# w_down of a ConvFFN by Strassen's seven block products for 16 of its 22 k tiles, and whole rows of x in the opening

## The chip, the cores and the metric

The kernel runs on one core of a Trainium2 chip. The metric is the device time of one execution in microseconds (us), lower is better. PE is the matmul engine (TensorE), DVE the VectorE, ACT the ScalarE, POOL the GpSimd, and SP the engine that issues the DMAs. PSUM has 8 banks here, each 128 partitions by 512 float32.

## What is computed

One decoder block on x of 512 tokens by 1024, in float32. Attention with a top-k choice and a recurrence run side by side, are merged and added to x; then comes a convolutional feed-forward part (FFN), and a last normalisation. The part that the change is about:

```python
    h = h + ga1 * jnp.dot(merged, w_out[l])
    xn = rms_norm(h, g_ffn[l]) * (1.0 + sc2) + sh2
    up = causal_dwconv(jnp.dot(xn, w_up[l]), conv_ffn_w[l], conv_ffn_b[l])
    val, gte = jnp.split(up, 2, axis=-1)
    h = h + ga2 * jnp.dot(jax.nn.silu(gte) * val, w_down[l])
return rms_norm(h, g_final)
```

w_up is 1024 by 5632 and w_down 2816 by 1024, so w_down has 22 tiles of 128 rows (k tiles).

## The kernel before, in words

**Number format.** Each float32 operand of a large product is split into a high part (an ACT copy to the matmul's type) and a low part (a DVE subtraction of that copy): `split`. A product is then three matmul passes, high by high, high by low and low by high (`mm3`, L530). A pass of 128x512 is the unit of work on PE in this text. Tiles with an h at the end of the name are high parts, with an l low parts (`wh`, `wl`; `dh`, `dl`; `acth`, `actl`).

**Order.** The program is recorded as operations with costs and ranks. A planner (`Plan.order`) lists them greedily by rank within a fixed number of slots for each kind of buffer, and writes out a fixed order for each engine. The engines then run these orders and wait for each other by semaphores. There are 3 slots of 1 MB for raw weights ("W"), 6 for split weights of 128x1024 ("w"), 75 tiles of 128x512 ("t") and the 8 banks ("b"). Everything that is loaded or stored goes through SP's queue in the planner's order.

**Opening.** x comes in as eight half rows of 256 KB (four row tiles `x`, two halves each), with the first block of w_ada (`wa`) between them. The squares of rows 2 and 3 go to ACT, the rows are scaled (`xs`), transposed on PE (L542), modulated, and multiplied with the first tiles of w_in (`w0h`, `w0l`). `WARM` groups of four transposes of the unit matrix stand on PE ahead of that. The modulation comes from dot products of w_ada with `crow`, one DVE instruction of 128x1024 each (L615).

**Middle.** w_in in tiles of 128 columns (8 k tiles, 24 passes each), attention, recurrence, w_o, w_out. `h1`, the residual after w_out, stays in SBUF as eight tiles (`xr_`).

**FFN.** Tile n of w_up (44 tiles, 22 loads of 1 MB, one for two tiles) is split (`wh`, `wl`), takes 24 passes of PE, and its bank goes through an ACT copy and two DVE multiply-adds for the convolution (`cv`, L471). A pair of tiles ends in a silu, a product, and the split into `acth` and `actl`. Behind the last tile, w_down runs k tile by k tile over eight banks (four row tiles t, two halves h): each load of 1 MB (`wd`) holds two k tiles, is multiplied by the gate `ga` on DVE, and split into `dh` and `dl`. The last five k tiles run bank by bank, so that the banks end one behind the other; the last bank is cut in two halves of 256 columns. Then each bank is added to h1, squared, scaled and stored.

Of the kernel before, what the change touches and what calls it, by code (L numbers as in the profile page):

```python
# [43 lines left out]
INFLATE = 1.19  # L44
HORIZON = 26
EARLY = 3
LAST = 5
# [4 lines left out]
WARM = 8  # L52
DOT1 = 13.6
SECOND = -25.0
LATER = 19.39
CLOCK = 12.7
RB = [3.28, 5.94, 7.96, 11.0, 13.85, 0.61]
SOON = [20.62, 17.45, 25.0, 11.19]
ISTEP = {1: 13, 2: 37.5, 3: 88.8}
IW = {1: 18, 2: 46.8, 3: 42.2}  # L60
ASTEP = {0: 76, 1: 93, 2: 126, 3: 145}
AW = [8, 13.5, 18.7, 30.4]
BUMP = [0.16, 0.81]
# [109 lines left out]
class Plan:  # L173
# [21 lines left out]
    def op(self, engs, reads, writes, emit, func=None, hold=(), n=1, tag="", follow=None):  # L195
# [25 lines left out]
        bufs += hold  # L221
# [15 lines left out]
    def order(self):  # L237
# [30 lines left out]
        table = [None]  # L268
# [127 lines left out]
def block_kernel(ctx: ExitStack, tc: tile.TileContext, x, cols, wada1, wada2, win0, win, wgate,  # L396
# [46 lines left out]
    def dma(dst, src, nbytes, reads=()):  # L443
        P.op({"sp": max(0.15, nbytes / 360e3)}, list(reads), [dst],
             lambda e: nc.sync.dma_start(real(dst), src() if callable(src) else src))

    def act(dst, src, func, bias=0.0, scale=1.0, accum=None, hold=()):
        n = width(src)
        cost = 0.04 + 0.00094 * n + 0.093 * sum(isinstance(v, (Buf, View)) for v in (bias, scale, accum))
# [12 lines left out]
    def tt(dst, a, b, op, engs=("dve",)):  # L462
        n = max(width(a), width(b))
        c = {"dve": 0.07 + 0.00104 * n, "pool": 0.03 + 0.00234 * n}
# [8 lines left out]
    def ts(dst, a, s1, s2, op0, op1=None, engs=("dve",)):  # L473
# [3 lines left out]
             "pool": 0.05 + 0.0014 * n}  # L477
# [96 lines left out]
    xt = [[t2(name="x") for _ in range(2)] for _ in range(TT)]  # L574
    for t in range(TT):
        for h in range(2):
            P.soft = -70.0 + 2 * t + h if t < 2 else -56.0 + 2 * t + h
            dma(xt[t][h], x[t * 128:(t + 1) * 128, h * 512:(h + 1) * 512], 1 << 18)
# [3 lines left out]
    for h in range(2):  # L582
# [4 lines left out]
        act(crow[:, h * 512:(h + 1) * 512], ps, AF.Copy)  # L587
    P.soft = None

    def rstd_of(halves, engs=("act", "dve")):  # L590
        parts = [small((128, 1), "ss") for _ in halves]
        ms = small((128, 1), "ms")
        for h, v in enumerate(halves):
            square(t2(name="junk")[:, :width(v)], v, parts[h], engs)
# [9 lines left out]
    def normed(halves, after=0.0, engs=("act", "dve")):  # L604
        r = rstd_of(halves, engs)
# [36 lines left out]
    xs = [normed(xt[t], LATER, ("act", "dve") if t < 2 else ("act",)) for t in range(TT)]  # L642
# [15 lines left out]
    for n in range(WARM):  # L658
        P.soft, P.after = -43.0, 3.7
        transposes(g0ps[-1], [ident] * 4)  # L660
    P.soft, P.after = None, 0.0
    n0 = len(G0) * 128
    for kt in range(KT):
        raw = buf("W", (128, 2, 1024), F32, "wa")
        if kt < 2:
            P.soft = -60.0 + 20.0 * kt
            dma(raw[:, 1, :], wada1[kt, :, 1, :], 1 << 19)
            P.soft = -58.0 + 20.0 * kt
            dma(raw[:, 0, :], wada1[kt, :, 0, :], 1 << 19)
# [446 lines left out]
    for t in range(TT):  # L1116
# [14 lines left out]
        h1.append(hv)  # L1131
# [23 lines left out]
    for n in range(2 * FT):  # L1155
        if n % 4 == 3 and ada_next < 16:
            ada_rest(ada_next)
            ada_next += 1
# [178 lines left out]
```

## Time and profile before

| | us |
|---|---|
| Median of 3 runs | 796.47 (796.18 to 796.88) |
| Profiled execution | 796.1 |
| Its span in the trace | 794.3 |
| First matmul of w_in starts, from the span's start | 17.34 |
| w_down's passes, alone on PE | 667.6 to 787.7 |

Columns "PE" and "PEld" are the matmuls and their weight loads, which overlap; matmuls are pipelined, so the duration of one is longer than the distance from its start to the next one's. The granted clock is a share of 2.4 GHz, TensorE's upper level; 0.50 is the lower one, 1.2 GHz. 1.8 us of the profiled execution lie outside the span.

### The profile page before, as it was taken

How to read it: one execution, taken by the hardware profiler on the slowest of the kernel's cores; microseconds unless marked ns; L12 is line 12 of the kernel's file. 1: busy time of each engine (PE TensorE's matmuls, PEld its weight loads, DVE VectorE, ACT ScalarE, POOL GpSimd, SP SyncE). 2: the span in 40 equal slices, each digit the busy share in tenths (PEclk: the TensorE clock that was granted, in tenths of full speed). 3: DMA queues.
4: the chain of work that ended last, by engine and by line, in shares of the span. 5: the costliest groups of instructions: out<-in, count | busy, mean ns of one | idle time of the engine just before them, and what ended most of it. 6: DMA issues, size and time to landing. Idle time of an engine off the chain costs nothing.

```text
span 794.3 us, 9871 instructions
## 1 busy us (share of the span) xinstructions
PE 775.3 (98%) x3608; PEld 645.3 (81%) x3608; DVE 595.8 (75%) x1144; ACT 439.2 (55%) x752; POOL 48.3 (6%) x69
## 2 busy tenths in 40 slices
PE   5999999999899999999999999999999999999996
PEld 5888888877777888888888888888888888888885
DVE  4997976999999998869866876665565698774034
ACT  6579935588799879635146644444444355232013
POOL 1000000014022051000010000000000000000000
PEclk8999999999999999999999999999999999999999
DMA  9974132321122451549740444333333224441002
GB/s 320 398 261 146 53 115 98 112 101 54 53 81 84 155 179 61 186 138 365 279 145 1 160 158 157 116 111 122 107 106 106 91 72 156 159 146 38 2 28 79
DMA packets 21298, 105.23 MB, mean 132 GB/s; under 512 B 2377, under 2 KB 4865, under 8 KB 10625
## 3 DMA queue, kind: packets, MB, share of 16 engines
q1 hardware_dynamic: 21248, 104.60, 36.6%
q8 instruction: 28, 0.46, 0.2%
q14 instruction: 22, 0.17, 0.1%
HBM read 102.47 MB, written 3.69 MB: 134 GB/s over the span
## 4 chain that ended last, share of the span: by engine, by line
PE 79%; DVE 11%; ACT 5%; issue 2%; DMA 1%; SPq 0%; POOLq 0%; POOL 0%; DVEq 0%; ACTq 0%
PE ps L530 78%; DVE sc L897 2%; DVE wl L466 2%; PE ps L542 2%; DVE m L896 1%; ACT l L459 1%; DVE sc L471 1%; DMA x<-in_x_dram 1%; ACT L459 1%; DVE h L854 1%; DVE q L471 1%; DVE rg L466 1%; ACT wh L459 1%; ACT gb L459 0%; DVE al L466 0%
## 5 line engine op out<-in xcount | busy, mean ns | idle before, releaser
L530 PE MATMUL ps<-yl,wh 128*128 128x512 f32 (+1 forms) x376 | 141.9, 377 | 0.3
L530 PE MATMUL ps<-yh,wh 128*128 128x512 f32 (+1 forms) x376 | 141.5, 376 | 0.0
L530 PE MATMUL ps<-yh,wl 128*128 128x512 f32 (+1 forms) x376 | 141.2, 375 | 0.0
L459 ACT ACTIVATE wh<-wr 128x1024 fp32r<-128x1024 f32 (+1 forms) x96 | 97.7, 1020 | 60.6 <-PE ps L530 46.6
L466 DVE TENSOR_TENSOR wl<-wr,wh 128x1024 fp32r<-128x1024 f32 (+1 forms) x96 | 113.1, 1179 | 21.6 <-ACT wh L459 21.5
L530 PE MATMUL ps<-xh,wl 128*128 128x512 f32 x288 | 112.4, 390 | 1.1 <-DVE wl L466 1.1
L530 PE MATMUL ps<-xh,wh 128*128 128x512 f32 x288 | 113.3, 394 | 0.0
L530 PE MATMUL ps<-xl,wh 128*128 128x512 f32 x288 | 112.3, 390 | 0.0
L471 DVE SCALAR_TENSOR_TENSOR cv<-ps,ct,cv 128x511 f32<-128x511 f32 x88 | 65.8, 748 | 48.3 <-ACT cv L459 47.1
L530 PEld LDWEIGHTS ps<-yl,wh 128*128 128x128 f32 x376 | 70.7, 188 | 14.0 <-DVE yl L466 1.1
L530 PEld LDWEIGHTS ps<-yh,wl 128*128 128x128 f32 x376 | 70.7, 188 | 12.9
L530 PEld LDWEIGHTS ps<-yh,wh 128*128 128x128 f32 x376 | 70.7, 188 | 12.8
L459 ACT ACTIVATE cv<-ps,ct 128x512 f32<-128x512 f32 x44 | 33.9, 770 | 74.8 <-PE ps L530 74.7
L530 PE MATMUL ps<-dl,acth 128*128 128x512 f32 (+1 forms) x181 | 69.3, 383 | 0.0
L530 PE MATMUL ps<-dh,actl 128*128 128x512 f32 (+1 forms) x181 | 69.3, 383 | 0.0
L530 PE MATMUL ps<-dh,acth 128*128 128x512 f32 (+1 forms) x181 | 69.3, 383 | 0.0
L530 PEld LDWEIGHTS ps<-xh,wl 128*128 128x128 f32 x288 | 54.1, 188 | 13.2 <-DVE wl L466 1.6
L530 PEld LDWEIGHTS ps<-xl,wh 128*128 128x128 f32 x288 | 54.1, 188 | 10.0
L530 PEld LDWEIGHTS ps<-xh,wh 128*128 128x128 f32 x288 | 54.2, 188 | 9.8
L615 DVE SCALAR_TENSOR_TENSOR wa<-wa,crow 128x1024 f32<-128x1024 f32 x48 | 57.8, 1221 | 4.9 <-DMA wa<-in_wada_dram 2.4
L459 ACT ACTIVATE dh<-wd 128x512 fp32r<-128x512 f32 x44 | 25.1, 622 | 36.4 <-PE ps L530 21.9
L466 DVE TENSOR_TENSOR dl<-wd,dh 128x512 fp32r<-128x512 f32 x44 | 29.0, 688 | 15.9 <-PE ps L530 14.1
(254 smaller groups left out, 1391.7 us busy)
## 6 DMA issues: line engine op xcount, KB each, us to landing
wa<-in_wada_dram SPq DMA_DIRECT2D x22, 1024.0 KB, 4.9
wr<-in_w_up_dram SPq DMA_DIRECT2D x22, 1024.0 KB, 4.8
wr<-in_win_dram SPq DMA_DIRECT2D x18, 1024.0 KB, 4.8
wd<-in_w_down_dram SPq DMA_DIRECT2D x11, 1024.0 KB, 4.8
wr<-in_wo_rnn_dram SPq DMA_DIRECT2D x4, 1024.0 KB, 6.0
wo<-in_w_out_dram SPq DMA_DIRECT2D x4, 1024.0 KB, 5.5
x<-in_x_dram SPq DMA_DIRECT2D x8, 256.0 KB, 6.2
wa<-in_wada_dram SPq DMA_DIRECT2D x4, 512.0 KB, 6.5
```

The costliest lines, as they stand in the source:

```text
L459: nc.scalar.activation(real(dst), real(src), func, **kw)
L466: lambda e: ENG[e].tensor_tensor(real(dst), real(a), real(b), op=op), tag="tt")
L471: lambda e: nc.vector.scalar_tensor_tensor(real(dst), real(a), real(s), real(b), op0=op0, op1=op1), tag="stt")
L530: nc.tensor.matmul(real(ps), real(a), real(b), start=st, stop=sp)
L542: nc.tensor.transpose(real(ps[:, i * 128:(i + 1) * 128]), real(s), real(ident))
L615: vop(1.14, [r, crow], [r, dst], lambda: nc.vector.scalar_tensor_tensor(real(r), real(r), 1.0, real(crow), op0=ALU.mult, op1=ALU.mult, acc ...
L854: vop(1.13, [a, u], [h], lambda h=h, a=a, u=u: nc.vector.tensor_tensor_scan(real(h), real(a), real(u), 0.0, op0=ALU.mult, op1=ALU.add))
L896: vop(0.065 + 0.00104 * W, [a], [m8], lambda m8=m8: nc.vector.max(real(m8), real(a)))
L897: vop(0.125 + 0.00104 * W, [a, m8], [a], lambda m8=m8: nc.vector.match_replace(real(a), real(m8), real(a), TAKEN))
```

## The change

For the first 16 k tiles of w_down (8 pairs of k tiles, in two slices of four pairs) the product is taken as a product of 2 by 2 blocks: two halves of the tokens (256 each) by two k tiles of a pair, and two k tiles by two halves of the columns (512 each). Strassen's scheme makes it from seven block products in place of eight; sums and differences of blocks are built first, on the activations (`as`, 128x256) and on w_down (`wd`, 128x512), and each product's result is added to or taken from up to two sums. One product m of a slice runs over four pairs and two banks (the two row tiles of a half of the tokens), three passes each, which makes 24 passes. It loads its one or two blocks of w_down again, as transfers of 256 KB. The two slices' 14 products stand in the program behind the up tiles that `SPREAD` names. The results are gathered in eight SBUF tiles `sum` (the first by an ACT copy, the others by DVE additions out of PSUM), which are multiplied by `ga` and added to the residual once. The last 6 k tiles run as before, all bank by bank, with the row tiles in the order 2, 3, 0, 1. The residual is stored to DRAM (`kept`) and read back (`h1`) before its addition. In the opening x comes as four whole rows of 512 KB, the two first blocks of w_ada as 1 MB each, DVE may take squares of all rows and copies half of `crow`; `WARM` is 12. The planner's costs and due times have new numbers.

```diff
-INFLATE = 1.19
+INFLATE = 1.03
-LAST = 5
+PAIRS = 8
+ORDER = [[4, 3, 0, 2, 1, 5, 6], [0, 1, 2, 3, 4, 5, 6]]
+ROWS = [2, 3, 0, 1]
+SLICES = [(0, 4), (4, 8)]
+SPREAD = [[17, 19, 21, 23, 25, 27, 29], [32, 34, 36, 37, 39, 41, 42]]
-WARM = 8
+WARM = 12
...
-    xt = [[t2(name="x") for _ in range(2)] for _ in range(TT)]
+    xt = [buf("w", (128, 1024), F32, "x") for _ in range(TT)]
     for t in range(TT):
-        for h in range(2):
-            P.soft = -70.0 + 2 * t + h if t < 2 else -56.0 + 2 * t + h
-            dma(xt[t][h], x[t * 128:(t + 1) * 128, h * 512:(h + 1) * 512], 1 << 18)
+        P.soft = (-80.0 if t < 2 else -58.0) + t
+        dma(xt[t], x[t * 128:(t + 1) * 128, :], 1 << 19)
...
-        act(crow[:, h * 512:(h + 1) * 512], ps, AF.Copy)
+        if h == 0:
+            act(crow[:, :512], ps, AF.Copy)
+        else:
+            vop(0.6, [ps], [crow[:, 512:]], lambda ps=ps: nc.vector.tensor_copy(real(crow[:, 512:]), real(ps)))
...
-    xs = [normed(xt[t], LATER, ("act", "dve") if t < 2 else ("act",)) for t in range(TT)]
+    xs = [normed([xt[t][:, 0:512], xt[t][:, 512:1024]], LATER) for t in range(TT)]
...
-            dma(raw[:, 1, :], wada1[kt, :, 1, :], 1 << 19)
-            P.soft = -58.0 + 20.0 * kt
-            dma(raw[:, 0, :], wada1[kt, :, 0, :], 1 << 19)
+            dma(raw, wada1[kt], 1 << 20)
...
-        h1.append(hv)
+            kept = buf("d", (128, 512), F32, "kept")
+            dma(kept, lambda v=xr_: real(v), 1 << 18, [xr_])
+            h1.append(kept)
...
+    def product(m, first, last):
+        lhs, rhs, sign, goes = PRODUCTS[m]
+        ps = [bank(2) for _ in range(2)]
+        for p in range(first, last):
+            raw = buf("W", (128, len(rhs), 512), F32, "wd")
+            for i, (kk, hh) in enumerate(rhs):
+                dma(raw[:, i, :], w_down[p, :, kk, hh * 512:(hh + 1) * 512], 1 << 18)
+            w = raw[:, 0, :]
+            if len(rhs) == 2:
+                tt(w, w, raw[:, 1, :], ALU.add if sign == 1 else ALU.subtract)
+            wh, wl = t2(F32R, name="dh"), t2(F32R, name="dl")
+            split(wh, wl, w)
+            v = [acts[2 * p + kk][:, A if hh == 0 else B] for hh, kk in lhs]
+            if len(v) == 2:
+                o = t2(name="as")
+                tt(o[:, A], v[0], v[1], ALU.subtract if m in MINUS else ALU.add)
+                v[0] = o[:, A]
+            hl = t2(F32R, name="ahl")
+            split(hl[:, A], hl[:, B], v[0])
+            planned(6 * pass_us(512))
+            for e in range(2):
+                c, d = slice(128 * e, 128 * e + 128), slice(256 + 128 * e, 384 + 128 * e)
+                mm3(ps[e], hl[:, c], hl[:, d], wh, wl, p == first, p == last - 1)
+            P.fix = None
+        P.soft = clock[0] + SOON[3]
+        for i, j, sg in goes:
+            for e in range(2):
+                key = (2 * i + e, j)
+                if key not in total:
+                    assert sg == 1
+                    total[key] = t2(name="sum")
+                    act(total[key], ps[e], AF.Copy)
+                else:
+                    tt(total[key], total[key], ps[e], ALU.add if sg == 1 else ALU.subtract)
...
+    for t in ROWS:
+        for h in range(2):
+            kept, v = h1[2 * t + h], total[t, h]
+            back = t2(name="h1")
+            dma(back, lambda kept=kept: real(kept), 1 << 18, [kept])
+            tt(v, v, ga_b[1][h], ALU.mult)
+            tt(v, v, back, ALU.add)
```

Three places in the engines' orders. **PE in the opening**, from `crow`'s last matmuls to w_in's first one, before (`ident` alone is a transpose of the unit matrix, `xs` one of a row of x):

```order
L530 MATMUL ps_120<-ident_79,csil_98 128x128 x3
L530 MATMUL ps_129<-ident_79,csil_98 128x128 x3
L542 MATMUL ps_110<-ident_79 128x128 x28
L542 MATMUL ps_210<-ident_79,xs_137 128x128
L542 MATMUL ps_210<-ident_79,xs_146 128x128
L542 MATMUL ps_246<-ident_79,xs_235 128x128
L542 MATMUL ps_246<-ident_79,xs_237 128x128
L542 MATMUL ps_251<-ident_79,xs_137 128x128
L542 MATMUL ps_251<-ident_79,xs_146 128x128
L542 MATMUL ps_251<-ident_79,xs_235 128x128
L542 MATMUL ps_251<-ident_79,xs_237 128x128
L530 MATMUL ps_261<-xh_232,w0h_227 128x256
```

and now:

```order
L534 MATMUL ps_105<-ident_79,csil_96 128x128 x3
L546 MATMUL ps_139<-ident_79 128x128 x8
L546 MATMUL ps_157<-ident_79,xs_135 128x128
L546 MATMUL ps_157<-ident_79,xs_149 128x128
L546 MATMUL ps_139<-ident_79 128x128 x40
L546 MATMUL ps_254<-ident_79,xs_228 128x128
L546 MATMUL ps_254<-ident_79,xs_246 128x128
L546 MATMUL ps_259<-ident_79,xs_135 128x128
L546 MATMUL ps_259<-ident_79,xs_149 128x128
L546 MATMUL ps_259<-ident_79,xs_228 128x128
L546 MATMUL ps_259<-ident_79,xs_246 128x128
L534 MATMUL ps_267<-xh_220,w0h_239 128x256
```

Of the warming transposes 40 have moved behind the transposes of x's first two rows, and 8 stay ahead.

**PE at the first product**, behind w_up's tile 17. Before, the same kind of place is the end of the last up tile, where w_down begins:

```order
L530 MATMUL ps_1336_6163<-yl_984_4369,wh_1334_6088 128x512
L530 MATMUL ps_1336_6163<-yh_983_4355,wl_1335_6089 128x512
L530 MATMUL ps_1441_6218<-dh_1343_5997,acth_1094_4654 128x512
L530 MATMUL ps_1441_6218<-dl_1344_5998,acth_1094_4654 128x512
L530 MATMUL ps_1441_6218<-dh_1343_5997,actl_1095_4655 128x512
L530 MATMUL ps_1442_6227<-dh_1345_6018,acth_1094_4654 128x512
L530 MATMUL ps_1442_6227<-dl_1346_6019,acth_1094_4654 128x512
L530 MATMUL ps_1442_6227<-dh_1345_6018,actl_1095_4655 128x512
```

and now:

```order
L534 MATMUL ps_1181_5249<-yl_980_4391,wh_1179_5153 128x512
L534 MATMUL ps_1181_5249<-yh_979_4384,wl_1180_5154 128x512
L534 MATMUL ps_1183_5304<-dh_1186_5045,ahl_1189_4752 128x512
L534 MATMUL ps_1183_5304<-dl_1187_5046,ahl_1189_4752 128x512
L534 MATMUL ps_1183_5304<-dh_1186_5045,ahl_1189_4752 128x512
L534 MATMUL ps_1184_5316<-dh_1186_5045,ahl_1189_4752 128x512
L534 MATMUL ps_1184_5316<-dl_1187_5046,ahl_1189_4752 128x512
L534 MATMUL ps_1184_5316<-dh_1186_5045,ahl_1189_4752 128x512
L534 MATMUL ps_1183_5304<-dh_1191_5099,ahl_1194_4877 128x512
```

A product stands behind an up tile, three passes for each of two banks, then the next pair with new `dh`, `dl` and `ahl`.

**DVE**, at the last up tile of before:

```order
L471 SCALAR_TENSOR_TENSOR cv_1337_6222<-ps_1336_6163,ct_1_84,cv_1337_6222 128x511
L466 TENSOR_TENSOR dl_1364_6232<-wd_1360_6108,dh_1363_6231 128x512
L471 SCALAR_TENSOR_TENSOR cv_1337_6222<-ps_1336_6163,ct_1_84,cv_1337_6222 128x510
L466 TENSOR_TENSOR wd_1369_6194<-wd_1369_6194,ga_1178_5304 128x512
L466 TENSOR_TENSOR wd_1369_6194<-wd_1369_6194,ga_1179_5314 128x512
L466 TENSOR_TENSOR cv_1333_6171<-cv_1333_6171,cv_1337_6222 128x512
L466 TENSOR_TENSOR wd_1369_6194<-wd_1369_6194,ga_1178_5304 128x512
L466 TENSOR_TENSOR dl_1366_6266<-wd_1360_6108,dh_1365_6265 128x512
L466 TENSOR_TENSOR actl_1339_6270<-cv_1333_6171,acth_1338_6269 128x512
L466 TENSOR_TENSOR dl_1368_6277<-wd_1360_6108,dh_1367_6276 128x512
L466 TENSOR_TENSOR dl_1371_6284<-wd_1369_6194,dh_1370_6283 128x512
L466 TENSOR_TENSOR wd_1369_6194<-wd_1369_6194,ga_1179_5314 128x512
```

now, in the second slice of products:

```order
L470 TENSOR_TENSOR wl_1331_5796<-wr_1329_5718,wh_1330_5795 128x1024
L470 TENSOR_TENSOR cv_1275_5740<-cv_1275_5740,cv_1279_5782 128x512
L470 TENSOR_TENSOR wd_1340_5772<-wd_1340_5772 128x512
L470 TENSOR_TENSOR sum_1205_5359<-sum_1205_5359,ps_1280_5778 128x512
L470 TENSOR_TENSOR sum_1206_5378<-sum_1206_5378,ps_1281_5784 128x512
L470 TENSOR_TENSOR sum_1240_5535<-sum_1240_5535,ps_1280_5778 128x512
L470 TENSOR_TENSOR sum_1241_5546<-sum_1241_5546,ps_1281_5784 128x512
L470 TENSOR_TENSOR wd_1345_5803<-wd_1345_5803 128x512
L470 TENSOR_TENSOR dl_1342_5830<-wd_1340_5772,dh_1341_5829 128x512
L470 TENSOR_TENSOR ahl_1410_5818<-cv_1178_5257,ahl_1410_5818 128x256
L470 TENSOR_TENSOR dl_1347_5852<-wd_1345_5803,dh_1346_5851 128x512
L470 TENSOR_TENSOR ahl_1414_5833<-cv_1246_5592,ahl_1414_5833 128x256
```

and at the last up tile:

```order
L470 TENSOR_TENSOR sum_1205_5359<-sum_1205_5359,ps_1574_7209 128x512
L470 TENSOR_TENSOR sum_1206_5378<-sum_1206_5378,ps_1575_7217 128x512
L470 TENSOR_TENSOR dl_1632_7280<-wd_1628_7144,dh_1631_7279 128x512
L475 SCALAR_TENSOR_TENSOR cv_1599_7303<-ps_1598_7255,ct_1_84,cv_1599_7303 128x511
L470 TENSOR_TENSOR dl_1638_7292<-wd_1628_7144,dh_1637_7291 128x512
L475 SCALAR_TENSOR_TENSOR cv_1599_7303<-ps_1598_7255,ct_1_84,cv_1599_7303 128x510
L470 TENSOR_TENSOR sum_1208_5386<-sum_1208_5386,ga_1169_5417 128x512
L470 TENSOR_TENSOR sum_1205_5359<-sum_1205_5359,ga_1168_5408 128x512
L470 TENSOR_TENSOR cv_1573_7214<-cv_1573_7214,cv_1599_7303 128x512
L470 TENSOR_TENSOR sum_1208_5386<-sum_1208_5386,h1_1644_6873 128x512
L470 TENSOR_TENSOR sum_1205_5359<-sum_1205_5359,h1_1645_6929 128x512
L470 TENSOR_TENSOR actl_1640_7337<-cv_1573_7214,acth_1639_7336 128x512
```

Beside the up tile's `wl` and `cv` there now stand the sums of blocks (`wd`, `as`), their low parts (`dl`, `ahl`) and the additions out of PSUM (`sum` with `ps`); and the last up tile's `actl`, which the last k tiles need, stands behind the last additions, the gate and the residual.

## Rows read from the trace of the kernel before

**Rows 1.** Page, part 1: busy time, share of the span and instructions of each engine.

```profile
PE 775.3 (98%) x3608; PEld 645.3 (81%) x3608; DVE 595.8 (75%) x1144; ACT 439.2 (55%) x752; POOL 48.3 (6%) x69
```

**Rows 2.** Page, part 4: shares of the chain that ended last, by engine.

```profile
PE 79%; DVE 11%; ACT 5%; issue 2%; DMA 1%; SPq 0%; POOLq 0%; POOL 0%; DVEq 0%; ACTq 0%
```

**Rows 3.** Busy time of each engine in three stages; the columns are in the first line.

```profile
core 0: us, PE busy (x) PEld busy (x) DVE busy (x) ACT busy (x) POOL busy (x), PEclk, DMA share, GB/s
17.34:423.80 406.46, 402.15 (x1866) 332.76 (x1864) 357.57 (x756) 280.91 (x488) 42.05 (x52) 1.00 0.42 152
423.80:667.60 243.80, 243.53 (x1146) 204.14 (x1145) 169.59 (x259) 116.71 (x181) 0.55 (x1) 1.00 0.32 112
667.60:787.70 120.10, 120.10 (x545) 100.05 (x543) 59.68 (x102) 29.50 (x57) 1.64 (x3) 1.00 0.24 85
```

**Rows 4.** The same view over two stretches of 100 us with attention in them.

```profile
100.00:200.00 100.00, 98.60 (x451) 81.86 (x449) 87.83 (x166) 63.24 (x94) 12.65 (x15) 1.00 0.27 95
200.00:300.00 100.00, 97.09 (x456) 78.87 (x455) 97.15 (x246) 88.83 (x178) 27.21 (x34) 1.00 0.32 111
```

**Rows 5.** Instruction groups of the last stage on PE: count | busy us, mean ns | idle before.

```profile
L530 PE MATMUL ps<-dh,acth 128*128 128x512 f32 x171 | 66.5, 389 | 0.0
```

**Rows 6.** Timeline of PE in the last stage: start us, duration us, instruction.

```profile
668.07 0.39 PE L530 MATMUL ps<-dl,acth 128*128 128x512 f32 x1
...
670.34 0.39 PE L530 MATMUL ps<-dh,actl 128*128 128x512 f32 x1
```

**Rows 7.** Chain of waits at the opening: start us, duration us, what.

```profile
3.99 7.63 DMA x<-in_x_dram
...
11.65 2.06 ACT junk L498 x6
...
23.75 0.44 PE ps L542 x4
```

**Rows 8.** Busy time at the opening, in stretches of 2 us (columns as in rows 3).

```profile
4.00:6.00 2.00, 2.00 (x11) 2.00 (x11) 0.63 (x3) 0.60 (x2) 0.00 (x0) 1.00 1.04 308
...
10.00:12.00 2.00, 0.02 (x1) 0.00 (x0) 1.39 (x3) 0.93 (x3) 0.00 (x0) 1.00 1.04 402
...
14.00:16.00 2.00, 0.48 (x1) 0.18 (x1) 0.94 (x3) 2.00 (x6) 1.09 (x2) 0.50 1.03 408
```

**Rows 9.** Timeline of PE: the opening transposes.

```profile
6.58 3.22 PE L542 MATMUL ps<-ident 128*128 128x128 f32 x28
```

**Rows 10.** Timeline of PE: the first matmuls of w_in.

```profile
17.34 0.56 PE L530 MATMUL ps<-xh,w0h 128*128 128x256 f32 x1
17.69 0.41 PE L530 MATMUL ps<-xl,w0h 128*128 128x256 f32 x1
...
19.61 0.41 PE L530 MATMUL ps<-xl,w0h 128*128 128x256 f32 x1
...
19.99 0.28 PE L530 MATMUL ps<-xh,w0h 128*128 128x256 f32 x1
...
20.94 0.28 PE L530 MATMUL ps<-xh,w0l 128*128 128x256 f32 x1
```

**Rows 11.** Timeline of DVE: four instructions one behind the other.

```profile
641.21 0.69 DVE L466 TENSOR_TENSOR dl<-wd,dh 128x512 fp32r<-128x512 f32 x1
641.81 1.22 DVE L466 TENSOR_TENSOR wl<-wr,wh 128x1024 fp32r<-128x1024 f32 x1
642.95 0.74 DVE L471 SCALAR_TENSOR_TENSOR cv<-ps,ct,cv 128x511 f32<-128x511 f32 x1
643.61 0.68 DVE L466 TENSOR_TENSOR dl<-wd,dh 128x512 fp32r<-128x512 f32 x1
```

**Rows 12.** Timeline of DVE in the opening: one instruction of 256 columns, and its follower.

```profile
15.72 0.43 DVE L466 TENSOR_TENSOR xl<-xf,xh 128x256 fp32r<-128x256 f32 x1 [0.57 <-ACT xh L459]
16.06 0.68 DVE L466 TENSOR_TENSOR w0l<-w,w0h 128x512 fp32r<-128x512 f32 x1
```

**Rows 13.** DMA view: issues by line, KB each, median us from issue to landing.

```profile
wd<-in_w_down_dram SPq DMA_DIRECT2D x11, 1024.0 KB, 4.8
...
w<-in_win_dram SPq DMA_DIRECT2D x8, 256.0 KB, 7.6
...
gf<-in_rows_dram SPq DMA_DIRECT2D x2, 256.0 KB, 3.0
```

## What the change should do to the time

> **What bounds the kernel now.** I read the page's first part, then the chain, then the busy time by stage. PE is busy for 98% of the span [rows 1] and holds 79% of the chain [rows 2]. By stage [rows 3] the FFN up to its last up tile has PE at 243.53 of 243.80 us, and w_down has it at 120.10 of 120.10, with DVE at 59.68 and ACT at 29.50. In w_down no pass waits [rows 5], and passes start at a fixed distance: ten starts behind 668.07 the timeline is at 670.34 [rows 6], 0.227 us each. So in these two stages a pass that is not made is time that is not spent, as long as the others keep up. Only two places have PE waiting. At the opening it stands nearly still until the first matmul at 17.34 [rows 8, 10]. In the attention stretch it loses 1.40 us between 100 and 200, and 2.91 between 200 and 300 with DVE busy for 97.15 [rows 4]: 4.3 us that DVE costs.
>
> The sum is made against the profiled execution: 796.1, which is the span plus 1.8; the median, 796.47, is 0.4 away, which I leave out.
>
> **Passes taken away.** w_down took 22 k tiles by 8 banks by 3 passes, 528 whole passes, all at 0.227. For 16 k tiles that is 384. The products need 14 x 4 pairs x 2 banks x 3 = 336. The 48 that go are 48 x 0.227 = **-10.9 us**. That the 336 do stand in PE's order is plain from it, so "the change doesn't do it" is no case. Unlike the old passes they stand between up tiles, where DVE and ACT still have `wl`, `cv` and the silus to make.
>
> **What DVE must do for it.** This is the term with the most risk. Durations from start to start: a 128x512 subtraction 0.60, `wl` 1.14, a `cv` multiply-add 0.66 [rows 11]; 256 columns 0.34 [rows 12]. From PE's first product to the `actl` of the last up tile, DVE's order has 184 instructions of 128x512, 25 `wl`, 55 multiply-adds and 78 of 256 columns: 110.4 + 28.5 + 36.3 + 26.5 = 202 us. PE has 26 up tiles x 24 + 336 + 33 passes of the last k tiles there, 993 x 0.227 = 225.4 us. DVE is at 90%. By the recorded durations in place of the distances (0.69, 1.22, 0.74 and 0.43) it would be 127 + 30.5 + 40.7 + 33.5 = 232 us, more than PE has: that is the upper bound, 6 us late. I take the distances, because rows 11 show DVE going at them without a gap. Going through the order, DVE stays 10 us or more ahead between the products. It gets tight at the end: from the end of the second last product to the last up tile's `actl` DVE has 38 rows, some 22.6 us, and PE 24 + 24 + 24 + 35 passes, 24.3 us. The lead is 1.7 us, and one late ACT copy eats it. I book **+1 us** for FFN stalls, with 0 and +6 as its ends. ACT has 116.71 of 243.8 busy before [rows 3]; it makes 56 `dh` in place of 32, 56 `ahl` in place of 16 `acth`, and 8 copies of banks. Even at DVE's 0.60 and 0.34 these are under 30 us more over a stage that is longer by 76; ACT is no bound.
>
> **What the loads must do.** The products read 96 blocks of 256 KB in place of 8 loads of 1 MB. The three W slots serve both these and w_up. In the second slice a product has 4 pairs and about 1.43 up tiles, 24 x 2.43 passes = 13.2 us, so 39.7 slot-us. It needs four slots for the time of landing plus some 2.8 us (addition, copy, subtraction and the wait for their turn), and 0.71 of a w_up load for about 13 us. A landing of 256 KB was 3.0 us for g_final and 7.6 for w_in in the crowded opening [rows 13]. At 3.9, nearer to the quiet row since the FFN's DMA share was 0.32 [rows 3], it is 26.8 + 9.2 = 36 of 39.7. That holds. With the blocks the core moves about 40 MB in the 225 us, 180 GB/s where it had 112, and the share should rise to about 0.5 to 0.6. This is hidden; at the high end of the landing it is a rival below. The stores of the residual and its return are 16 more transfers of 256 KB on SP, with `kept` ahead of a few weight loads there; the first reader is in the tail, hundreds of us later, and 0.5 us of issue each is covered by loads that are issued early. Nothing. For PSUM a product holds two of eight banks until DVE's additions; they stand at once behind it. Nothing.
>
> [...]
>
> **Opening.** The first matmul waits for the last rows of x: the transfer lands at 11.62, then ACT makes six squares' worth of work in 2.06 us [rows 7]. While half rows come in, DMA moves 308 GB/s at a share of 1.04; later, with other shapes, 402 at the same share [rows 8]. Over the 5.5 us in which they flow, 94 GB/s are 0.5 MB, 1.3 us at 400. A square on DVE takes 0.7 off ACT's row. The first matmul then starts at 15.3. Then the clock. PE has the granted clock 0.50 at 14 to 16 after its idle stretch [rows 8], and the first twelve passes of w_in take 2.65 us from 17.34 to 19.99, where eight later ones take 0.95 [rows 10]. Now 40 transposes stand behind x's first rows in PE's order; 28 took 3.22 [rows 9], so 40 take 4.6 and reach from about 9.6 to 14.2. With PE busy there, I expect the upper level: 12 x (0.221 - 0.119) = 1.2 us. That makes 3.2 at the first k tile's end. DVE's dot products of 1.22 us for the second k tile do not get earlier by all of that, and I give back 0.7: **-2.5 us**. Its ends are 0 (DVE and the loads set the pace of the second k tile, whose transposes stood at 23.75 [rows 7]) and -4.
>
> [...]
>
> **Middle.** The order gives DVE two 128x512 multiplications fewer in the attention stretch (`rg`, now on POOL) and shuffles the rest. Two by 0.60 are 1.2 us less where DVE is the bound: **-1.5 us** with what the earlier opening leaves. Ends: -4.3, all that PE idles [rows 4], and +2, if the new order meets one wait that the old one avoided. The end behind the last matmul is as it was, 6.6 us.
>
> 796.1 - 10.9 - 2.5 - 1.5 + 1 = **782.2 us**.
>
> **Rivals.**
> DVE is the bound: by the upper bound above, or by ACT and DVE waiting for each other in the chains of addition, copy and subtraction that each pair needs. Then +6 to +9 in place of +1: 787 to 791, say 789. For it: 90% is close, and DVE at 97% cost PE 2.9 us in 100 [rows 4]. Against it: at 85 to 90% (87.83 of 100 in rows 4) PE lost only 1.4, and the loads can be made early. 0.14.
>
> The W slots are the bound, the slower side. If blocks of 256 KB land in 7.6 us [rows 13], the second slice needs 4 x 10.4 + 9.2 = 50.8 slot-us of 39.7, 3.7 us for each product, 26 in all; the first slice, at 16.3 us for each product, loses 1.6 seven times, 11. Less the lead of 13 us PE is 24 late: 805. It ends slower than before once 13 us or more of stall are added, from a landing of about 7.0 us on. For it: w_in's row has just that size. Against it: there the DMA share was 1.0, and here it is about half. 0.07.
>
> PE's pipeline isn't what the passes cost, and 48 fewer give nothing: then 793.1. Against it: the steady 0.227 with no idle [rows 5, 6]. 0.03. The Trainium skill speaks for it: "Perfetto Trace Analysis", Identifying the Most-Contended Engine, calls matmul busy time a bad metric and judges by the weight loads' busy share, which is 81% here [rows 1]. That reads as 19% of headroom on PE; the trace's fixed distance of starts disagrees.
>
> **How the numbers follow.** My forecast has 0.76, the DVE case 0.14, the slots 0.07, idle gains 0.03. The forecast's own ends are 796.1 - 10.9 - 4 - 4.3 = 777 and, with 0 for the opening, +2 in the middle and +1, 788; with the DVE case beside it 777 to 791 leaves out the slots, the last rival and some tails, under 2 in 10. A measurement of this kernel can tell 0.2% from no change, 1.6 us. Faster holds the first two cases and the last one, 0.91 with something off for what I haven't seen; within 0.2% is 0.03, slower 0.06.
>
> **What would show it.** Right: w_up and the products in one stretch of PE without idle of over 1 us, passes at 0.227, some 48 fewer; DVE about 90% there; 256 KB blocks in 3 to 5 us; the clock at 1.00 when the first matmul of w_in starts, at about 15.3; PE idle of about 3 us from 100 to 300. Wrong: PE waiting for `dl`, `ahl` or `actl` (DVE), for `wd` through DVE's addition (loads), for a bank behind `sum`, or a half clock at the first matmuls because 40 transposes came too late.

## The result and the profile after

The changed kernel takes **790.99 us** (median of 4 runs, 790.10 to 791.86) against 796.54 before: a ratio of 0.9925, 95% interval 0.9913 to 0.9938. That is 5.5 us less. I had forecast 782.2, 14.3 less. The profiled execution took 790.1, its span 788.3. It is 6.0 us shorter than the span of before, so the two traces hold the result. They are one execution each, and two executions of one of the kernels below lie up to 9 us apart, so a difference of one microsecond between two traces shows nothing by itself.

The page of the changed kernel, its parts 1 and 4, answers to [rows 1, 2]:

```profile
PE 768.4 (97%) x3579; PEld 639.7 (81%) x3579; DVE 666.9 (85%) x1315; ACT 461.4 (59%) x815; POOL 50.5 (6%) x72
...
PE 54%; DVE 24%; DMA 12%; issue 4%; ACT 4%; SPq 0%; POOLq 0%; POOL 0%; DVEq 0%; ACTq 0%
```

PE's busy time fell by 6.9 us, not by 11, and PE's share of the chain fell from 79% to 54%: DVE and the loads of w_down now stand in it.

The three stages of [rows 3]: up to w_up, then w_up with the products, then w_down alone. The view is the busy time by stretch, its columns in the first line.

```profile
core 0: us, PE busy (x) PEld busy (x) DVE busy (x) ACT busy (x) POOL busy (x), PEclk, DMA share, GB/s
15.93:423.85 407.92, 403.02 (x1868) 333.78 (x1866) 356.23 (x758) 279.54 (x490) 44.27 (x55) 0.99 0.43 156
423.85:743.08 319.23, 319.13 (x1482) 267.08 (x1481) 274.46 (x477) 160.47 (x279) 0.55 (x1) 1.00 0.50 173
743.08:782.00 38.92, 35.43 (x163) 28.82 (x161) 26.19 (x49) 11.61 (x26) 1.64 (x3) 0.96 0.11 41
```

The middle stage is what was hoped for: 319.13 of 319.23 us busy with 336 passes more in it. The last stage is not: PE is idle for 3.5 of 38.92 us, and its granted clock is 0.96 in the mean. The first stage has 4.9 us of PE idle, before it had 4.3, and a clock of 0.99.

PE's waits behind the first 30 us, by what ended them: us in total, times, the longest.

```profile
PE ps L534 <- ACT acth L463: 3.0, 1, 3.0
PE ps L534 <- DVE q L475: 2.9, 2, 2.0
...
PE ps L534 <- DVE actl L470: 0.4, 1, 0.4
```

The milestones of both timelines on PE, from the span's start, give the ledger:

| First pass of | before | after | gain so far |
|---|---|---|---|
| w_in, first k tile | 17.34 | 15.93 | 1.41 |
| w_in, first tile by whole k (`wh`) | 60.47 | 58.97 | 1.50 |
| attention's first `kh` by `q` | 197.61 | 195.42 | 2.19 |
| recurrence's output (`rh`) | 306.49 | 302.86 | 3.63 |
| w_out (`woh`) | 378.68 | 377.56 | 1.12 |
| w_up (`yh`) | 424.02 | 423.85 | 0.17 |
| w_down alone (`acth`) | 667.85 | 743.08 | |
| last pass of all | 787.60 | 781.78 | 5.82 |

(Between `rh` and `woh` the two orders place the passes differently, so the two middle rows don't compare one to one; those at 424 do.) By 424 us only 0.2 us of the opening's gain is left. In the profiles of tail_order, one_block and fill_ahead, which have the same order up to there, w_up starts at 424.33 to 424.99, so there none is left. From there on 5.65 us are won. The 48 passes are worth 10.9 in that stretch, the waits and the clock at the tail take 5.9 back, and w_up with the products ran 0.8 shorter than 243.8 + 336 x 0.227 = 320.0.

**The tail.** The timeline of PE around the first passes that need the last up tile (start, duration, instruction; in brackets the idle time before it and what ended it):

```profile
750.75 0.40 PE L534 MATMUL ps<-dh,actl 128*128 128x512 f32 x1
754.10 0.50 PE L534 MATMUL ps<-dh,acth 128*128 128x512 f32 x1 [2.95 <-ACT acth L463]
...
755.24 0.72 PE L534 MATMUL ps<-dh,actl 128*128 128x512 f32 x1 [0.41 <-DVE actl L470]
755.76 0.63 PE L534 MATMUL ps<-dh,acth 128*128 128x512 f32 x1
...
758.75 0.41 PE L534 MATMUL ps<-dl,acth 128*128 128x512 f32 x1
759.00 0.40 PE L534 MATMUL ps<-dh,actl 128*128 128x512 f32 x1
```

Thirty-three passes run first: thirty of the tail's first two banks and three of the third. Then PE waits 2.95 us for `acth` and 0.41 for `actl`, and behind that the passes start 0.43 us apart in place of 0.227, until 758.75. (Of the passes in between, some are left out.) From 749.20 to 759.00 there are 17 steps, 3.85 us at the usual distance; they took 9.80. So the tail costs **5.9 us** in this execution: 3.4 of waits, some 1.7 of passes that start 0.4 to 0.5 us apart behind the second wait, and the rest of smaller delays.

DVE in the same stretch:

```profile
744.16 0.69 DVE L470 TENSOR_TENSOR sum<-sum,ga 128x512 f32<-128x512 f32 x1
...
745.97 0.69 DVE L470 TENSOR_TENSOR sum<-sum,h 128x512 f32<-128x512 f32 x1
...
747.77 1.28 DVE L470 TENSOR_TENSOR sum<-sum,ps 128x512 f32<-128x512 f32 x2
...
749.57 0.75 DVE L475 SCALAR_TENSOR_TENSOR cv<-ps,ct,cv 128x511 f32<-128x511 f32 x1
...
750.83 0.74 DVE L475 SCALAR_TENSOR_TENSOR cv<-ps,ct,cv 128x510 f32<-128x510 f32 x1
751.49 1.28 DVE L470 TENSOR_TENSOR sum<-sum,ga 128x512 f32<-128x512 f32 x2
...
753.29 1.29 DVE L470 TENSOR_TENSOR sum<-sum,h 128x512 f32<-128x512 f32 x2
754.50 0.69 DVE L470 TENSOR_TENSOR actl<-cv,acth 128x512 fp32r<-128x512 f32 x1
```

and ACT, where the copy of the last up tile's bank stands:

```profile
747.35 0.63 ACT L463 ACTIVATE dh<-wd 128x512 fp32r<-128x512 f32 x1 [1.17 <-DVE wd L470]
747.89 0.76 ACT L463 ACTIVATE cv<-ps,ct 128x512 f32<-128x512 f32 x1
```

The last up tile's passes end at 743.25. ACT copies the bank only at 747.89, since three `dh` stand ahead of it that wait for DVE, and DVE makes the two multiply-adds at 749.57 and 750.83, behind a gate and a residual (at 744.16 and 745.97) and two additions out of PSUM (747.77) that nobody needs yet. Four more such rows (751.49 and 753.29) stand in between before `actl`. From the full bank to the end of `actl` it took 11.9 us; I had given it 8 (35 passes). In all that time DVE itself waits for nothing: from 730.21 on it runs without a gap.

**The stretch before it.** DVE came into the tail late. Three of its rows, 20 to 40 us earlier:

```profile
713.68 1.23 DVE L470 TENSOR_TENSOR wl<-wr,wh 128x1024 fp32r<-128x1024 f32 x1 [3.42 <-ACT wh L463]
...
725.85 0.69 DVE L470 TENSOR_TENSOR wd<-wd 128x512 f32<-128x512 f32 x1 [0.99 <-DMA wd<-in_w_down_dram]
...
732.02 1.28 DVE L470 TENSOR_TENSOR sum<-sum,ps 128x512 f32<-128x512 f32 x2
```

The first wait of 3.42 us is for ACT's `wh`, and the chain of waits names what that waits for, a load of w_up that takes 7.47 us to land (the median is 5.0) and is issued as soon as DVE has finished an earlier `wl`:

```profile
703.94 1.14 DVE wl L470
705.10 7.47 DMA wr<-in_w_up_dram
```

The third row shows how late DVE was. These are the additions out of the second last product's banks, whose last pass ended at 726.9 on PE; DVE makes them at 732.0, 5.1 us later.

### The profile page after: what moved, and what is told of

The parts are those of the page before. It is cut to its first block, busy times and chain, and to the rows that moved or that the text cites. A ratio compares the mean times of both kernels' runs of the same rounds, so it can differ in the third digit from the quotient of the medians.

```text
span 788.3 us, 10204 instructions
## 1 busy us (share of the span) xinstructions
PE 768.4 (97%) x3579; PEld 639.7 (81%) x3579; DVE 666.9 (85%) x1315; ACT 461.4 (59%) x815; POOL 50.5 (6%) x72
## 4 chain that ended last, share of the span: by engine, by line
PE 54%; DVE 24%; DMA 12%; issue 4%; ACT 4%; SPq 0%; POOLq 0%; POOL 0%; DVEq 0%; ACTq 0%
PE ps L534 53%; DMA wd<-in_w_down_dram 7%; DVE dl L470 3%; DMA wr<-in_w_up_dram 3%; DVE wl L470 3%; DVE sum L470 3%; DVE cv L475 2%; DVE wd L470 2%; DVE wa L621 2%; DMA wa<-in_wada_dram 2%; PE ps L546 2%; ACT wh L463 1%; DMA wo<-in_w_out_dram 1%; DVE ahl L470 1%; DVE sc L901 1%
## 5 line engine op out<-in xcount | busy, mean ns | idle before, releaser
L463 ACT ACTIVATE dh<-wd 128x512 fp32r<-128x512 f32 x68 | 42.5, 630 | 78.0 <-DVE wd L470 69.9
L475 DVE SCALAR_TENSOR_TENSOR cv<-ps,ct,cv 128x511 f32<-128x511 f32 x88 | 65.6, 745 | 11.9 <-ACT cv L463 11.2
L534 PE MATMUL ps<-dh,ahl 128*128 128x512 f32 x224 | 71.3, 389 | 0.0
L534 PEld LDWEIGHTS ps<-dh,ahl 128*128 128x128 f32 x224 | 42.0, 188 | 8.7
L470 DVE TENSOR_TENSOR dl<-wd,dh 128x512 fp32r<-128x512 f32 x68 | 45.8, 684 | 3.4 <-ACT dh L463 3.1
L534 PE MATMUL ps<-dl,ahl 128*128 128x512 f32 x112 | 43.6, 389 | 0.0
```

The lines of the kernel that those rows point to most:

```text
L463: nc.scalar.activation(real(dst), real(src), func, **kw)
L470: lambda e: ENG[e].tensor_tensor(real(dst), real(a), real(b), op=op), tag="tt")
L475: lambda e: nc.vector.scalar_tensor_tensor(real(dst), real(a), real(s), real(b), op0=op0, op1=op1), tag="stt")
L534: nc.tensor.matmul(real(ps), real(a), real(b), start=st, stop=sp)
```

## The experiments

In the edits below `move` takes operations out of the finished order and puts them, in the same sequence, in front of (0) or behind (1) another; `find` gets operations by engine and tile names. No planner runs anew, so nothing else changes its place. The first row of the table has its own session, with 796.54 for the kernel before; in the sessions of the others that was 796.89 to 796.93. So where two medians are 2 us apart or less, the ratios and their intervals are the better guide.

| Kernel | median us | ratio to before, interval |
|---|---|---|
| the change | 790.99 | 0.9925 (0.9913 to 0.9938) |
| tail_order | 786.63 | 0.9888 (0.9863 to 0.9913) |
| fill_ahead | 786.35 | 0.9871 (0.9858 to 0.9884) |
| one_block | 785.85 | 0.9868 (0.9854 to 0.9883) |
| no_products | 795.93 | 0.9994 (0.9983 to 1.0004) |
| q_first | 788.17 | 0.9902 (0.9871 to 0.9933) |
| yr_on_pool | 788.65 | 0.9886 (0.9859 to 0.9912) |
| before_pool | 794.76 | 0.9974 (0.9966 to 0.9983) |
| no_warm | 790.79 | 0.9925 (0.9910 to 0.9940) |
| tail_and_pool | 783.74 | 0.9826 (0.9809 to 0.9844) |
| all_three | 782.13 | 0.9816 (0.9804 to 0.9829) |

### The tail: DVE's order

```diff
+    last = find("dve", "actl_1640")[0]
+    late = [o for o in find("dve", "sum_") if at(o) < at(last)][-8:]
+    move(late, last, 1)
```

> The changed kernel with one edit: eight DVE instructions (gate and residual of sums of rows 2, 3 and 0, and the last product's two additions out of PSUM) stand behind the last up tile's actl instead of ahead of it. Theory A (DVE's order at the tail is the cause: those 4.8 us of work stand ahead of the last up tile's multiply-adds): PE's wait of 3.0 + 0.4 us at 751 to 755 falls under 1 us, the half clock behind it goes, about 4.5 us less, 786.5. Theory B (ACT's order is the cause, its copy of the last bank stands behind dh copies that wait for DVE): the wait stays over 2 us and the time within 2 us of 791. Theory C (DVE is late because loads starve it upstream): a gain of a part, 2 to 4 us.

Measured: 786.63, 4.4 less than the change by the medians and 2.9 by the ratios. Four of its six runs took 785.5 to 787.4 and two 791.0 and 791.8, no less than the change; what happened in these two no trace shows. PE's waits behind 30 us, in the profile of this kernel:

```profile
PE ps L534 <- DVE q L475: 3.1, 3, 2.0
PE ps L534 <- DVE wol L470: 0.8, 1, 0.8
PE ps L534 <- DVE wl L470: 0.5, 1, 0.5
```

`acth` and `actl` are gone from the list, and the granted clock is 1.00 from 745 to 763. Theory A holds, B falls: ACT's copy was late because its `dh` waited for DVE.

### The tail: the loads

```diff
-                dma(raw[:, i, :], w_down[p, :, kk, hh * 512:(hh + 1) * 512], 1 << 18)
+                k = 4 if i else 512
+                ... dma_start(raw[:, i, 0:k], w_down[p, :, kk, hh * 512:hh * 512 + k])
...
-                tt(w, w, raw[:, 1, :], ALU.add if sign == 1 else ALU.subtract)
+                ... tensor_tensor(w, w, w, op=ALU.add)
```

> The changed kernel in the same order; the second block of each pair that adds two blocks of w_down is left out of the load (16 bytes a row in place of 2 KB), and the addition takes the first block twice: 40 of the 96 loads of 256 KB are gone, no instruction is. Theory C (loads through three W slots starve DVE, 13.1 us of waits for wd and 6.3 for wl, and so it is late at the tail): these waits fall under 8 us in all, and PE's wait at the tail falls under 1 us, about 785.5. Theory A (the order at the tail alone): DVE's waits fall, the tail's wait stays over 2.5 us, 790 to 791.

Measured: 785.85. DVE's waits from 500 to 760, in the changed kernel:

```profile
DVE wd L470 <- DMA wd<-in_w_down_dram: 13.1, 15, 1.7
DVE wl L470 <- ACT wh L463: 6.3, 6, 3.4
```

and in this one:

```profile
DVE cv L475 <- ACT cv L463: 14.8, 10, 2.9
DVE wl L470 <- ACT wh L463: 3.7, 8, 0.7
...
DVE wd L470 <- DMA wd<-in_w_down_dram: 0.7, 1, 0.7
```

13.1 us of waits for `wd` became 0.7, 6.3 for `wl` 3.7, and PE's tail has no wait left. DVE now waits for the banks instead (14.8 us for ACT's `cv`): it runs ahead of PE and has to stop. So theory C holds too. In these traces both had to come together: without the loads' waits DVE arrives early enough for the poor order, and with a good order it can afford to arrive late. This kernel doesn't say whether the three W slots or the landings make the waits. The change's own trace points to the slots: between 440 and 757 us SP, ready to issue, waits 83.9 us in all for `dl` and 69.0 us for `wl`, with which DVE reads a raw block for the last time. A fourth slot would show it, and it wasn't tried.

### The tail: other work for PE

```diff
+    move([find("pe", "ps_1659", a)[0] for a in ("acth_1613", "acth_1620", "acth_1626", "acth_1633")],
+         find("pe", "ps_1649", "acth_1639")[0], 0)
```

> The changed kernel with one edit on PE alone: twelve passes of the tail's third bank, whose operands are all there, stand ahead of the six passes of the first two banks that need the last up tile's acth and actl. DVE's and ACT's orders are untouched. Theory A (only the time at which actl is ready counts, and 12 passes x 0.227 = 2.7 us of other work stand ready): PE's wait of 3.0 + 0.4 us falls to about 0.7, the half clock behind it goes or gets shorter, 786 to 787.5. Rival (DVE falls behind by as much elsewhere, the low parts or the banks are late): time within 1.5 us of 791.

Measured: 786.35. No wait is left behind 500 us in its profile, and the clock stays at 1.00 there. Twelve passes, 2.7 us, covered waits of 3.4, and the slow passes went with them: 4.6 us for an edit in which DVE and ACT do the same as in the change.

The traces give the price of the tail without the opening's spread. From w_up's first pass to the last pass of all PE takes 357.9 us in the change, and 352.3, 352.0 and 352.0 in tail_order, one_block and fill_ahead; before it took 363.6, and 48 passes less make 352.7. DVE needs 15.2 us from the start of one `actl` to the start of the last one in each of the six traces with the change's DVE order at the tail, and 12.3 in the three where the eight rows stand behind it. How much of that PE has to wait for depends on when PE arrives: in no_warm and q_first, whose order at the tail is the change's, w_up starts at 425.4 and 425.1 in place of 423.85, and the same stretch takes 354.0 and 356.7.

### Opening and middle without the products

The edit is the whole change except for w_down and the residual's way through DRAM; on every engine the order up to w_out is the changed kernel's.

> The kernel before with everything of the change but w_down: opening, planner's costs and numbers as changed; w_down's 22 k tiles and the residual in SBUF as before. Its order is the changed kernel's on every engine up to w_out. Theory F (opening gains 1.8 us and the attention stretch gives nearly all back by PE's wait for q and the half clock behind it): within 0.5 us of the kernel before, 796. By the terms of the prediction (-2.5 and -1.5): 792.5. If the products themselves disturb the opening or the middle: under 795.

Measured: 795.93 against 796.89 before in the same session, 0.9994 with 1 in the interval. Theory F: opening and attention stretch together bring nothing that can be measured. The products bring the rest: 795.93 - 790.99 = 4.9 us, or 5.5 by the ratios; the traces' terms, 10.9 and 0.8 less the tail's 5.9, make 5.8.

### The middle: which order, or how much work

In the changed kernel's trace PE stands here from 195.5 to 199.3:

```profile
195.47 0.28 PE L534 MATMUL ps<-kl,q 128*128 128x128 f32 x1
197.76 0.30 PE L534 MATMUL ps<-kh,q 128*128 128x128 f32 x1 [2.01 <-DVE q L475]
...
199.33 0.45 PE L534 MATMUL ps<-kh,q 128*128 128x128 f32 x1 [0.93 <-DVE q L475]
...
205.38 0.59 PE L534 MATMUL ps<-xl,wh 128*128 128x512 f32 x1
```

and DVE, in the same stretch, makes four scans (`h`), the four multiplications of `yr` by `h`, and then `q`:

```profile
188.25 5.23 DVE L858 TENSOR_TENSOR_SCAN h<-a,rg 128x512 f32<-128x512 f32 x4
193.40 2.97 DVE L470 TENSOR_TENSOR yr<-yr,h 128x512 f32<-128x512 f32 x4
...
196.87 3.09 DVE L475 SCALAR_TENSOR_TENSOR q<-ps,ct,q 64x512 fp32r<-64x512 f32 x4
```

Before, PE came to this place at 197.67 and waited 0.93 us for `q`; now it comes at 195.47, and DVE's multiplications end at 196.4 in place of 197.6. PE is 2.2 us early for a DVE that is 1.2 early, and has four `q` ahead of the next step where there were two.

```diff
+    move([o for n in ("q_486", "q_487", "q_492", "q_493") for o in find("dve", n)],
+         find("dve", "yr_268", "h_")[0], 0)
```

> The changed kernel with one edit: four DVE evictions of q stand ahead of the four multiplications yr by h instead of behind them. Theory D (PE's 2.9 us wait for q near 195 to 200 and the half clock after it come from this order alone): wait under 1 us, granted clock 1.00 from 186 to 212, and 3 us less at the end, about 788. Theory E (DVE bounds the whole stretch from 180 to 300, and what PE is early there it gives back): the wait moves to a later place before 300, the time within 1 us of 791.

Measured: 788.17, with an interval of 0.9871 to 0.9933 that holds the change's own ratio. PE's waits in its profile:

```profile
PE ps L534 <- DVE wl L470: 4.0, 1, 4.0
PE ps L534 <- ACT acth L463: 2.1, 1, 2.1
```

The waits for `q`, 2.9 us, are gone, and a wait of 4.0 us for the next `wl` stands there, where it was 0.4. The profile shows theory E: DVE has so much to do there that an instruction moved ahead moves another behind, and w_up starts at 425.11, no earlier than in the change. The time alone would not tell D from E: the median is what D forecast, and the six runs lie between 786.2 and 795.5.

```diff
+    on_pool = [find("dve", n, "h_")[0] for n in ("yr_268", "yr_288", "yr_412", "yr_434")]
+    for o in on_pool:
+        o.eng = "pool"
+    move(on_pool, find("pool", "bm_558")[0], 1)
```

> The changed kernel with one edit: the four multiplications yr by h (128x512, 3.0 us on DVE from 193.4 to 196.4) run on POOL, behind its addition bm_558; their readers come after 280 us. Theory E (DVE's amount of work bounds the stretch from 180 to 202, as moving q ahead only moved the wait): PE's waits for q and wl there fall from 3.3 us to under 1.5, the half clock there gets shorter or goes, and the time is 2 to 4 us less, 787 to 789. Rival (DVE shares its port with POOL, or POOL's bm are late and DVE waits for them): waits of the same sum, time within 1 us of 791.

Measured: 788.65, 2.3 less (3.1 by the ratios, whose intervals nearly touch). The busy time by stretch in the change (last three columns: granted clock, DMA share, GB/s)

```profile
196.00:202.00 6.00, 2.88 (x11) 2.07 (x12) 5.84 (x10) 2.22 (x3) 0.96 (x1) 0.75 0.00 0
202.00:208.00 6.00, 6.00 (x19) 4.77 (x20) 5.84 (x19) 3.26 (x10) 0.73 (x1) 0.68 0.00 0
```

and in this kernel

```profile
196.00:202.00 6.00, 4.68 (x24) 3.56 (x24) 5.87 (x15) 3.52 (x7) 4.75 (x4) 1.00 0.00 0
202.00:208.00 6.00, 6.00 (x28) 4.68 (x27) 5.91 (x22) 4.16 (x13) 1.06 (x2) 1.00 0.25 71
```

The granted clock stays at 1.00 where the change has 0.75 and 0.68, and w_up starts at 419.95 in place of 423.85: 3.9 us won by 2.4 to 3.0 us of DVE work taken away. But the three longest of PE's waits in this kernel are

```profile
PE ps L534 <- ACT acth L463: 3.0, 1, 3.0
PE ps L534 <- DVE dl L470: 1.5, 2, 0.8
PE ps L534 <- DVE wl L470: 1.0, 1, 1.0
```

The tail takes 2.2 of the 3.9 us back: PE comes to its first passes there 3.9 us earlier than in the change, DVE's last `actl` (752.31 for 754.50) only 2.2.

> The kernel before with the same edit alone: yr by h on POOL. If DVE bounds the stretch in the kernel before as well (4.3 us of PE idle there): 1.5 to 2.5 us less than before, 794 to 795. If its waits hang on single instructions: within 0.5 us of before.

The same edit on the kernel before (its four tiles have other numbers): 794.76, 0.9974 (0.9966 to 0.9983), 2.2 us less. PE's waits for `q` and `wl` of the kernel before, 0.9 and 1.1 us, are gone from its list. So DVE bounded this stretch before the change as well, as [rows 4] say.

### The opening's 40 transposes

```diff
+    warm = [o for o in find("pe", "ident") if o.tag == "tr" and len(o.bufs) == 2 and o.n == 4 and at(o) > at(find("pe", "xs_")[0])][:10]
+    for o in warm:
+        seq.remove(o)
```

> The changed kernel without the 40 transposes of the unit matrix that stand behind x's first rows. Theory G (they keep the clock up and cost nothing, since x's last rows are scaled only at 14.9): the first matmul stays at 15.7 to 16.2, the granted clock is 0.50 there, the first twelve passes take 2.6 us in place of 1.5, and the time is about 1.2 us more, 792. Rival (the 40 transposes, which end at 15.0, hold up the first matmul): it starts earlier, at 15 or before, and the time is the same or less.

Measured: 790.79, the same as the change. In its trace of PE

```profile
16.61 0.56 PE L534 MATMUL ps<-xh,w0h 128*128 128x256 f32 x1
...
19.31 0.41 PE L534 MATMUL ps<-xh,w0h 128*128 128x256 f32 x1
...
23.55 0.48 PE L534 MATMUL ps<-xh,w0h 128*128 128x512 f32 x1
```

the first matmul is at 16.61, where the change has it at 15.93. The passes are at half clock, 0.21 us apart (eleven rows left out), and the second k tile's first matmul comes at 23.55, where the change has its at 22.2.

This is one execution, at 787.75 the fastest of its six, and neither theory covers what the traces show. The eight profiles of changed kernels that keep the 40 transposes fall into two groups. In five the transposes took 4.53 us and the first matmul came at 15.69 to 16.68. In three (fill_ahead, q_first, tail_and_pool) the clock was 0.50 in the stretch from 12 to 14 us, the transposes took 6.20 us, the transposes of x's last rows followed without a wait, and the first matmul came at 17.38 to 17.45, later than without them. So they cost nothing that shows where the clock is up, as theory G says, and hold up the first matmul where it isn't, as the rival says. The second k tile's first matmul came at 21.94 to 22.93 in all eight, earlier than in no_warm. The time doesn't show that either; this fits the loss of the opening's gain in no_products.

### Together

> The changed kernel with both edits that took a wait away: the eight DVE instructions behind the last actl, and yr by h on POOL. If the two losses are independent: 786.6 - 3 = 783.6, and PE's waits after 30 us under 3 us in all. If what PE gains in the middle is given back in the products (DVE or W slots late by as much): no less than 785.5.

Measured: 783.74, as if the two were independent (4.4 and 2.3 of 791.0 leave 784.3). That the sum fits is partly luck, for in its trace they aren't: w_up starts 3.75 us earlier than in the change, but from there to the last pass PE takes 355.4 us, 3.1 more than in tail_order. What is left in its list of PE's waits is again mainly the tail:

```profile
PE ps L534 <- ACT acth L463: 2.8, 1, 2.8
PE ps L534 <- DVE wl L470: 1.0, 1, 1.0
```

> The changed kernel with eight DVE instructions behind the last actl, yr by h on POOL, and the twelve passes ahead. The kernel with the first two had 783.74 and still waits 2.8 us for the last acth. With the passes ahead that wait is covered: 780.5 to 781.5. If DVE and the loads are what is late in all of the tail: over 783.

Measured: 782.13, ratio 0.9816. With the twelve passes ahead no wait is left at the tail. It misses its forecast by 0.6 us; `wol`, at w_out, waits 1.7 in that profile. This version beats the change by 8.9 us and the kernel before by 14.8.

## Why the prediction was wrong, step by step

- **Passes.** Right. 48 passes at 0.227 are 10.9 us, and w_up with the products ran without a gap. The rival that PE's pipeline would make them free is out. It was the one that the Trainium skill would have supported ("Perfetto Trace Analysis", Identifying the Most-Contended Engine): by the weight loads' busy share, 81% before and after, there would be headroom in both kernels; the fixed distance of 0.227 us in both says there is none.
- **DVE in the FFN, +1 us.** This term failed: it measured 5.9 us less the 0.8 that the products' stage gained. The step was the lead at the tail, "The lead is 1.7 us, and one late ACT copy eats it". The count of rows was right: 38 rows for 22.6 us, and they took 23.2, from 732.0 to the end of `actl` at 755.2. The start was wrong. I let DVE begin them when the second last product ends, and it began 5.1 us later, because the loads had made it wait, 3.42 and 0.99 us shortly before. So a lead of 1.7 us became a lag of 3.4, which is what PE waited. No late ACT copy was needed: behind 730.2 DVE never waited for ACT. And I gave a wait only its own length, while slow passes and smaller delays cost 2.5 us more. The end of +6 that I took from the recorded durations was met by accident: over the whole stage DVE was not the bound, since PE was busy for 100.00 of 100 us both from 500 to 600 and from 600 to 700, with DVE at 84.45 and 91.89.
- **Loads.** The landing of a block of 256 KB was booked at 3.9 us; the row of after has a median of 3.4:

```profile
wd<-in_w_down_dram SPq DMA_DIRECT2D x96, 256.0 KB, 3.4
```

  PE never waited for a block. But "That holds" was said of PE only. DVE waited for them, 13.1 us in all, and those waits used up DVE's lead, as one_block shows, where they are gone and PE doesn't wait.
- **Opening, -2.5 us.** The mechanism held in this execution: the clock was 1.00 at the first matmul, at 15.93 for a forecast of 15.3, and the second k tile's transposes came at 21.97 for 23.75. But 1.8 us at that place are not 1.8 us at the end. In three other profiles of changed kernels the transposes ran at half clock and the first matmul came no earlier than before (17.38 to 17.45 for 17.34). What whole rows of x bring by themselves no run shows, since the blocks of w_ada changed with them.
- **Middle, -1.5 us.** It measured +1.3 between 60 and 424 us in the trace. The faulty step, the second one, is that opening and middle were added as if independent. A stretch that DVE bounds doesn't start earlier for a PE that comes earlier; no_products shows the sum of both at 0.9994. The order there also made PE's single wait longer, and the slow passes followed. Taking work off DVE did help, as the term said: 2.3 us in yr_on_pool, 2.2 in before_pool. The change's two `rg` on POOL were not tested by themselves.
- **End.** 6.5 us behind the last matmul's start for 6.7 before: right.
- **Range and rivals.** 790.99 lies just at the upper end of the range, near the DVE rival's 789, and that is in part luck: the rival's own +9 adds up to 790.2, not to 791. Its place was wrong too: not the products but the tail and the attention stretch. The W slot rival needed landings of 7.0 us, and 3.4 put it aside as a bound of PE through the products. (Its loss in the first slice, 1.6 us for each product, comes to 1.9 with one w_up load of 13 us.)

The sum as it came, in the two traces: -10.9 for the passes, -0.8 in the products' stage, -1.5 for the opening, +1.3 in the middle, +5.9 at the tail, and about 0 for the end: -6.0, and 794.3 became 788.3. The forecast had -13.9. Of the 7.9 us between, 4.1 are DVE's term and 3.8 opening and middle.

## What to carry to other kernels

When work is taken off the busiest engine, look for the last value that the second engine must deliver to it, follow that value through every engine's queue, and count what stands ahead of it that nobody needs yet; here eight instructions moved were worth as much as 13 to 19 matmul passes (2.9 us by the ratios, 4.4 by the medians). A gain in front of a stretch that another engine bounds is no gain: add the terms of a sum only when nothing between them waits. And a wait of PE can cost more than its length, by the slow passes behind it; here that was so in some executions and not in others.

## What the runs showed of the hardware

The clock was dearer than I had expected in the middle of the kernel. In the changed kernel PE waited 2.01 and 0.93 us between 195.5 and 199.3, and behind that most passes were 0.43 us apart, while PE was at work: from 200.2 to 205.4 ten steps took 5.2 us in place of 2.3, of which 0.4 was a wait. At the tail it was the same behind 2.95 and 0.41 us. In no_warm a tail wait of 1.1 and 0.4 us was followed by no half clock, nor was the wait of 2.8 us at the tail of tail_and_pool (1.00 from 745 to 757). In q_first the half clock behind a wait of 4.0 us in the attention stretch was half as long as in the change (0.72 from 202 to 208, where the change has 0.75 and 0.68 from 196 to 208), and behind 2.1 and 0.4 us at the tail it was as long; so one profile tells whether it fell, not whether it always will. What decides it I leave open. The opening shows the same spread: under the same order the first matmul came at 15.93 in the change's profile, 15.75 in tail_order, 17.45 in tail_and_pool and 18.64 in no_products, the last two with the clock at 0.50 from 12 to 14 us. The times spread as well: the six runs of yr_on_pool lie between 782.6 and 790.3. Whether that comes from the clock only a trace of each run would show.
